# First product of the first FFN: twelve column tiles as six units of seven half-size products, and the last gate's adaLN columns computed in the last FFN

## The chip, the cores and the metric

The kernel runs on one core of a Trainium2 chip, in one launch. The metric is device time in microseconds of that core. The median of three runs of the kernel before is 1328.9 us (1328.61 to 1329.11).

## The reference, cut to what matters

A sequence of 512 tokens with 1024 features passes two layers. Each layer is a token mixer (a short convolution in layer 0, an SSD mixer in layer 1) followed by a SwiGLU FFN. All four sub-layers have RMSNorm before and after, and a shift, a scale and a gate that come from the condition vector `c`:

```python
mod = (jax.nn.silu(c) @ ada_w + ada_b).reshape(bsz, DEPTH, 2, 3, D_MODEL)
...
shift, scale, gate = (mod[:, i, 1, k][:, None, :] for k in range(3))
h = rmsnorm(x, norm_g[i, 2]) * (1.0 + scale) + shift
y = swiglu_ffn(h, f_w_in[i], f_w_out[i])
x = x + gate * rmsnorm(y, norm_g[i, 3])

def swiglu_ffn(h, w_in, w_out):
    gate, up = jnp.split(h @ w_in, 2, axis=-1)
    return (jax.nn.silu(gate) * up) @ w_out
```

`w_in` of an FFN is 1024 x 5632: 22 gate tiles and 22 up tiles of 128 columns. `ada_w` is 1024 x 12288; its last 1024 columns (from `88 * P`) make the gate of the last FFN.

## The kernel before, in words

**Numbers.** Every large product is float32 made of three matmuls. An operand is split into a rounded part ("hi", ScalarE: `act.copy` into float32r) and the rest ("lo", VectorE: a subtraction), and the product is hi*hi + hi*lo + lo*hi. A weight tile of 128 columns (1024 x 128) costs one hi of 128x1024 and one lo of 128x1024, and, as a plain product (`in_chunk`, `mm_chunk`, `mm3`, L279 to L281), 8 k-tiles x 3 = 24 matmuls of 128x512.

**First FFN, first product** (L1152 and on; `up`, `gate`, `load_pair`). Six column tiles are begun while `h` is being formed and ended by `rest(0..5)`. Then a loop over k = 0 to 37 computes one column tile at a time: `load_pair` loads two tiles with one DMA of 1 MB two rounds ahead, `in_chunk(ws[k], h)` is its 24 matmuls, `gate` is a Silu on ScalarE, `up` multiplies on VectorE, `splits[k + 2]` makes hi and lo of the tile after next, and `sums(n)` runs n steps of the adaLN sums. A finished row tile lies in `raw`; `low_parts` forms sums of halves for the second product.

**adaLN columns.** The columns of `ada_w` that are not needed at the start are summed on VectorE beside the products. `ada_begin(n)` takes n sets of 512 columns, each in four loads of 512 KB (`ada_load`, `SP` queue, three buffers). `sums(1)` is one step: `ada_madd` (L125 for the first of a set, L127 for the others), one multiply-add of 128x512; a set has eight, and after them one `ada_fold` (L134). After each pair of sets a small matmul with `four`, four short additions into `mods`, and for gates `put_gates` (a transpose, a copy, a DMA to memory). The first FFN takes 14 sets, so 112 steps; the last two are the gate of the last FFN.

**Last FFN, first product** (L1840 to L2190). It already has the form that the change brings to the first FFN. Tokens are halved into two times 256, the 1024 rows into two times 512, and two neighbouring column tiles form a unit: a 2x2 by 2x2 product of halves, done with seven products in place of eight. A product is 4 k-tiles x 3 = 12 matmuls of 128x256 (L1920). Even units are gate tiles, odd ones up tiles. A unit u has four weights:

- X: the first column tile, 8 k-tiles; used by P1 and P2.
- Y: sums of the column tiles' halves (`sg`, partly added by DMA, partly by `sum_y`); used by P5 and P6.
- Z: the second tile less or plus other halves (its sum by DMA); used by P7 and P4.
- S: a half-size sum (`sum_s`); used by P3.

Each has its hi on ScalarE (L1875) and its lo on VectorE (L1876). `fetch(u)` issues four or five loads on `SP` (L1859 to L1865) and two accumulating DMAs on `POOL` (`add_`, L1852): of `sg`, then of the Z part of the unit before. `tq` holds the token halves' sums, made once from `h` (`value`, `t_hi`, `t_lo`, `t_four`).

The order of one unit on PE, with v = u - 1, is P1(u), P7(v), P5(u), P2(u), P4(v), P6(u), P3(u). Beside it VectorE runs, in this order: `c12(v)` (L1937, and L1939 for odd v), lo of X(u+1), `c22(v)` (L1946), in some units one `s13` (L1827, L1828), `c11(u)` (L1933), lo of Z(u), `sum_y(u+1)` (L1899), `sum_s(u+1)` (L1903), for odd v the product of `c21` (L1954), lo of Y(u+1), lo of S(u+1). ScalarE runs the hi parts, the copies out of PSUM (L1930) and the Silu's (L1942 for even v, between `c12(v)` and hi of X(u+1)). `c22(v)` reads the PSUM bank A of unit v between P7(v), which it follows, and P4(v), which adds to the same bank: P4(v) waits for it.

**The order is written by hand.** Both parts stand under `tc.manual_schedule` for PE, SP, ScalarE, VectorE and GpSimd: each engine issues its instructions in the order of the code, and a waiting instruction holds all that stand behind it on that engine. The buffers: `wst_p` two (staged weights), `whl_p` four (split weights), four PSUM banks `mm_ps` (A and C of the units) and four `aux_ps` (B).

**The end** (L2200 to L2310). The second product of the last FFN runs over `parts`; `behind(n)` (L2230 and on) does what follows product n: at 31 it multiplies two tiles by the gate (`gated`, L2219), at 33 it reads the two A banks (L2246) that the next product overwrites.

Of the kernel before, what the change touches and what calls it, by code (L numbers as in the profile page):

```python
# [16 lines left out]
P = 128  # L17
# [21 lines left out]
def trunk_kernel(  # L39
# [89 lines left out]
    ada_p = []  # L129

# [441 lines left out]

    ada_sets = []
    for q0 in (16, 0 + 24, 8 + 24, 16 + 24, 48, 56, 64, 72, 80, 88):
        ada_sets += [q0 * P, q0 * P + 512]
# [4 lines left out]
    with ExitStack() as ph:  # L580
# [5 lines left out]
        pool.tensor_tensor(four[:, 0:64], ident[:, 0:64], ident[:, 64:128], ADD)  # L586
        pool.tensor_tensor(four[:, 64:96], four[:, 0:32], four[:, 32:64], ADD)
        pool.tensor_copy(four[:, 0:32], four[:, 64:96])
        pool.tensor_copy(four[:, 32:64], four[:, 64:96])
        pool.tensor_copy(four[:, 96:128], four[:, 64:96])  # L590
# [378 lines left out]
        ffp = ph.enter_context(tc.tile_pool(name="ffp", bufs=NF - NS, reuse_waits="tile"))  # L969
        st_p = ExitStack()  # L970
        sa = st_p.enter_context(tc.tile_pool(name="sa", bufs=1, reuse_waits="tile"))
        wx = [sa.tile([P, 2, 2, T], F32, tag=f"wx{u}", name="w2x") for u in range(3)]
        s1t = sa.tile([P, NS // 2, 256], F32, tag="s1t", name="s1t")
        raw = [sa.tile([P, 4, T], F32, tag=f"raw{q}", name=f"raw{q}") for q in (3, 2, 1, 0)][::-1]
        lead_p = []
# [32 lines left out]

        def up(f, pst):
            g = gates[f]  # L1010
            if f < NS:
                dve.tensor_mul(raw[f // 4][:, f % 4, :], pst, g)
                if f % 4 == 3:
                    p = f // 2 - 1
                    lows.append(lambda: dve.tensor_tensor(a_("s1", p, 2), a_("a21", p, 2), a_("a22", p, 2), SUB))
                    lows.append(lambda: dve.tensor_tensor(a_("a21", p, 2), a_("a11", p, 2), a_("a21", p, 2), SUB))
                return
            a = acts[f] = ffp.tile([P, 2, T], F32R, tag="a", name=f"ff{f}")
# [4 lines left out]
        def low_parts():  # L1023
            while lows:
                lows.pop(0)()

# [125 lines left out]
        with tc.manual_schedule(engines={PE_ENGINE, mybir.EngineType.SP, mybir.EngineType.Activation,  # L1152
                                         mybir.EngineType.DVE, mybir.EngineType.Pool}):
            load_pair(0)
            madds = ada_begin(14)
            for i, f in ((0, 0), (2, 0), (1, 1), (3, 1), (4, 2), (5, 3)):
                rest(i)
                if i in (2, 3):
                    up(f, lead_ps[i])
                    sums(1)  # L1160
                    low_parts()
                else:
                    gate(f, lead_ps[i])
                sums(1)
# [3 lines left out]
            tiles = []  # L1168
            last = 2 * NF - 7
            for k in range(last + 1):  # L1170
                if k % 2 == 0 and k < 2 * NF - 10:
                    load_pair(k // 2 + 1)
                if k in (16, 20, 24):
                    x_load((k - 16) // 4)
                if k in (last - 2, last - 1):
                    xy_load(n_s - 2 + k - last + 2)
                tiles.append(in_chunk(ws[k], h))
# [3 lines left out]
                if j < 2 and k > 2:  # L1181
                    gate(4 + 2 * q + j, tiles[k - 1])
                elif k:
                    up(2 + 2 * q + j, tiles[k - 1])
                if k + 2 < len(splits):
                    for op in splits[k + 2]:
                        op()
                low_parts()
                sums(4 if j < 2 else 3)
                if k == 2 * NF - 12:  # L1190
                    ggs.append(make_gg(1, gg_tile))
                if k == last - 1:
                    assert next(madds, None) is None and not ada_sets and not quarters
# [12 lines left out]
            up(NF - 1, tiles[-1])  # L1206
            for step in todo:
                list(step)
            rows_g = [put_gates(q, mm_ps) for q in (2, 3)]
            for step in rows_g:  # L1210
                next(step)
# [15 lines left out]
            for q, item in enumerate(seq):  # L1227
# [6 lines left out]
                if q in (0, 5):  # L1234
                    list(rows_g[q // 5])
# [532 lines left out]
    with ExitStack() as ph:  # L1768
# [66 lines left out]
        def up(f, pst):  # L1835
# [5 lines left out]
        LO, HI = HALVES  # L1841
        FACTORS = {"P1": ("X", 0, "A"), "P2": ("X", 4, "B"), "P3": ("S", 0, "C"), "P4": ("Z", 4, "A"),
                   "P5": ("Y", 0, "C"), "P6": ("Y", 4, "A"), "P7": ("Z", 0, "A")}
        staged, wts, banks, outs = {}, {}, {}, {}

        def w1_cols(u, f, kh=None):
            c0 = u % 2 * DFF + (4 + u // 2 * 2 + f) * P
            rows = slice(0, D) if kh is None else slice(kh * T, (kh + 1) * T)
            return w1[rows, c0:c0 + P].rearrange("(k p) f -> p k f", p=P)

        def add_(dst, src):
            pool.dma_start(dst, src, accum_op=ADD)  # L1852

        def fetch(u):

            st, sg = wst_p.tile([P, 16, P], F32, tag="wst", name="wsu"), sums_w[:, u % 2]
            staged[u] = st, sg
            if u < UN:
                dma(sg[:, 0], w1_cols(u, 1, 0))  # L1859
                dma(sg[:, 1], w1_cols(u, 1, 1))  # L1860
            if u:
                dma(st[:, 8:12, :], w1_cols(u - 1, 1, 0))
            dma(st[:, 0:8, :], w1_cols(u, 0))
            if u:
                dma(st[:, 12:16, :], w1_cols(u - 1, 1, 1))  # L1865
            if u < UN:
                add_(flat2(sg[:, 0]), flat2(sg[:, 1]))
            if u:
# [462 lines left out]
```

## Time and profile before

| what | value |
|---|---|
| median of three runs | 1328.9 us |
| the profiled execution, its own time | 1328.93 us |
| its span, first to last instruction | 1327.1 us, clock 0.999 |
| PE busy | 1313.8 us, 99% of the span |
| VectorE busy | 1028.0 us, 77% |
| ScalarE busy | 641.5 us, 48% |
| first FFN, six begun tiles and loop | from about 229 to about 451 us |
| last FFN, its units | from 1029.88 us |

The profile is one execution recorded on the chip. PE is TensorE's matmuls, PEld its weight loads, DVE VectorE, ACT ScalarE, POOL GpSimd, SP the engine that issues most DMAs. Matmuls overlap each other, so the distance between two starts, not a matmul's own length, is what one costs; for the other engines too, the next start can lie a little ahead of an end. An entry in brackets tells how long the engine stood idle before the instruction and what ended the wait.

### The profile page before, as it was taken

Reading aid. Unit: us, or ns where it says so; the run is one execution under the profiler, and the core shown is the slowest. Engines: PE = TensorE matmul, PEld = TensorE weight load, DVE = VectorE, ACT = ScalarE, POOL = GpSimd, SP = SyncE. Lnnn points to the kernel's source line nnn. Section 1 sums busy time; section 2 is a strip of 40 time slices with the busy share of each in tenths; the row PEclk is TensorE's granted clock in tenths of the full one; section 3 lists DMA queues with packets and bytes.
Section 4 is the critical chain, followed back from the end, with each engine's and each line's share of the span. In section 5 each row is a group of like instructions: output and inputs, shape, how many; then the busy total and the mean of one; then the engine's idle time right before and its main releaser. Section 6 shows DMA issues by size and latency. Waiting matters only on the chain.

```text
span 1327.1 us, 19226 instructions
## 1 busy us (share of the span) xinstructions
PE 1313.8 (99%) x7437; PEld 1134.4 (85%) x7437; DVE 1028.0 (77%) x1654; ACT 641.5 (48%) x1042; POOL 85.9 (6%) x106
## 2 busy tenths in 40 slices
PE   8999999999999999999999999999999999999997
PEld 7788889888888888898888888888789999998886
DVE  5588866788776686769998989888678777766897
ACT  5322357222222465665554555554574555544665
POOL 0000000000000140000000000000000111101320
PEclk9999999999999999999999999999999999999999
DMA  9757760688885692414534243413252788878961
GB/s 312 230 191 226 247 228 1 214 267 259 286 292 195 178 180 65 130 34 147 159 111 134 74 143 112 143 64 127 85 154 53 190 216 209 200 194 287 177 119 64
DMA packets 203456, 222.21 MB, mean 167 GB/s; under 512 B 8788, under 2 KB 148964, under 8 KB 202340
## 3 DMA queue, kind: packets, MB, share of 16 engines
q1 hardware_dynamic: 186496, 184.74, 44.7%
q0 software_dynamic: 12720, 23.34, 10.2%
q10 hardware_dynamic: 4148, 12.90, 3.0%
q8 instruction: 58, 0.95, 0.3%
q14 instruction: 34, 0.28, 0.1%
HBM read 195.37 MB, written 2.24 MB: 149 GB/s over the span
## 4 chain that ended last, share of the span: by engine, by line
PE 93%; DMA 2%; SPq 2%; DVE 1%; ACT 1%; issue 1%; DVEq 0%; ACTq 0%
PE ip L279 15%; PE ip L281 14%; PE ip L280 14%; PE y L381 8%; PE sA L1920 7%; PE cA L2015 4%; PE cA L1127 3%; PE sC L1920 3%; PE li L279 3%; PE li L281 3%; PE li L280 3%; PE sB L1920 2%; PE li L767 1%; PE yd L1512 1%; PE cC L2015 1%; PE cD L2015 1%
## 5 line engine op out<-in xcount | busy, mean ns | idle before, releaser
L279 PE MATMUL ip<-h,whl 128*128 128x512 f32 x840 | 331.6, 395 | 0.2 <-DVE cv L874 0.2
L281 PE MATMUL ip<-h,whl 128*128 128x512 f32 x840 | 327.6, 390 | 0.0
L280 PE MATMUL ip<-h,whl 128*128 128x512 f32 x840 | 327.4, 390 | 0.0
L279 PEld LDWEIGHTS ip<-h,whl 128*128 128x128 f32 x840 | 157.8, 188 | 33.7 <-issue 1.8
L281 PEld LDWEIGHTS ip<-h,whl 128*128 128x128 f32 x840 | 157.7, 188 | 33.2
L280 PEld LDWEIGHTS ip<-h,whl 128*128 128x128 f32 x840 | 157.9, 188 | 31.7
L225 DVE TENSOR_TENSOR whl<-wst,whl 128x1024 fp32r<-128x1024 f32 x99 | 120.4, 1221 | 41.6 <-ACT whl L224 41.5
L224 ACT CAST whl<-wst 128x1024 fp32r<-128x1024 f32 x99 | 102.3, 1042 | 61.2 <-DMA wst<-in_f_w_in_dram 49.9
L127 DVE SCALAR_TENSOR_TENSOR ada_acc<-ada_st,csil,ada_acc 128x512 f32<-128x512 f32 x140 | 105.0, 750 | 21.5 <-DMA ada_st<-in_ada_w_dram 18.1
L381 PE MATMUL y<-whlo,ys 128*128 128x512 f32 x384 | 89.4, 392 | 0.0
L381 PEld LDWEIGHTS y<-whlo,ys 128*128 128x128 f32 x384 | 71.8, 188 | 15.8 <-issue 0.7
L279 PE MATMUL li<-h,whl 128*128 128x256 f32 x288 | 83.4, 290 | 0.0
L281 PE MATMUL li<-h,whl 128*128 128x256 f32 x288 | 81.7, 284 | 0.0
L280 PE MATMUL li<-h,whl 128*128 128x256 f32 x288 | 81.6, 283 | 0.0
L1920 PE MATMUL sA<-tq,whl 128*128 128x256 f32 x576 | 74.6, 284 | 0.3 <-DVE g L1946 0.3
L1920 PEld LDWEIGHTS sA<-tq,whl 128*128 128x128 f32 x576 | 71.6, 192 | 0.6 <-DVE g L1946 0.5
L1366 DVE SCALAR_TENSOR_TENSOR cu<-ip,cols,cu 128x511 f32<-128x511 f32 (+2 forms) x84 | 62.8, 747 | 4.0 <-ACT cu L1363 1.4
L2015 PE MATMUL cA<-whlo,ao 128*128 128x512 f32 x264 | 61.0, 391 | 1.2 <-ACT whlo L1980 1.0
L2015 PEld LDWEIGHTS cA<-whlo,ao 128*128 128x128 f32 x264 | 49.3, 188 | 12.3 <-ACT whlo L1980 2.0
L1876 DVE TENSOR_TENSOR whl<-wsu,whl 128x1024 fp32r<-128x1024 f32 x33 | 40.4, 1223 | 23.4 <-ACT whl L1875 23.4
L279 PEld LDWEIGHTS li<-h,whl 128*128 128x128 f32 x288 | 55.3, 192 | 0.0
L280 PEld LDWEIGHTS li<-h,whl 128*128 128x128 f32 x288 | 55.3, 192 | 0.0
(371 smaller groups left out, 2319.5 us busy)
## 6 DMA issues: line engine op xcount, KB each, us to landing
ada_st<-in_ada_w_dram SPq DMA_DIRECT2D x96, 512.0 KB, 5.9
wst<-in_f_w_in_dram SPq DMA_DIRECT2D x26, 1024.0 KB, 7.2
wst<-in_m_w_in_dram SPq DMA_DIRECT2D x14, 1024.0 KB, 5.4
wst<-in_m_w_in_dram SPq DMA_DIRECT2D x20, 512.0 KB, 6.0
wst<-in_a_w_in_dram SPq DMA_DIRECT2D x9, 1024.0 KB, 6.8
wsu<-in_f_w_in_dram SPq DMA_DIRECT2D x17, 512.0 KB, 5.5
csb<-cs_d ACTq DMA_DIRECT2D x8, 1024.0 KB, 6.5
sg<-in_f_w_in_dram SPq DMA_DIRECT2D x32, 256.0 KB, 3.4
```

Of the source, the lines that this page charges most:

```text
L127: dve.scalar_tensor_tensor(acc, w, csil[:, k:k + 1], acc, MUL, ADD)
L224: later.append((lambda sw=sw, w=w: act.copy(w[:, 0, :nk, :], sw), lambda sw=sw, w=w: dve.tensor_tensor(w[:, 1, :nk, :], sw, w[:, 0, :nk, : ...
L225: lambda sw=sw, w=w: dve.tensor_tensor(w[:, 1, :nk, :], sw, w[:, 0, :nk, :].bitcast(F32), SUB)))
L279: pe.matmul(dst, w_at(w, 0, kk), a[:, 0, sl], start=start, stop=False)
L280: pe.matmul(dst, w_at(w, 0, kk), a[:, 1, sl], start=False, stop=False)
L281: pe.matmul(dst, w_at(w, 1, kk), a[:, 0, sl], start=False, stop=stop)
L381: pe.matmul(pst, a[:, al, tk], wt[:, wl, kk, :], start=k == 0 and i == 0, stop=k == K - 1 and i == 2, skip_group_check=bool(held))
L1127: pe.matmul(bank[r, sub], a[:, al, q, tk], w[:, wl, q, :], start=first and k == 0, stop=False, skip_group_check=True)
L1366: dve.scalar_tensor_tensor(u[:, sft:], pst[:, :T - sft], w[3 - sft], u[:, sft:], MUL, ADD)
L1876: dve.tensor_tensor(dst[:, 1], src, dst[:, 0].bitcast(F32), SUB)
L1920: pe.matmul(dst, w[:, wl, k0 + k, :], moving(q, k, al), skip_group_check=True, start=q in ("P1", "P5", "P2") and k == 0 and i == 0, stop=k ...
L2015: pe.matmul(bank[r][sub], a[:, al, q, tk], w[:, hl, q, :], start=first and k == 0, stop=last and k == 2, skip_group_check=True)
```

## The change

It makes the functions of the last FFN's units into two classes, `Units` and `Values`, and uses them in the first FFN for the column tiles 4 to 9 of gate and up (12 tiles, 6 units, `UN1 = 6`); tiles 10 to 21 stay plain. In the first FFN each unit also holds two adaLN steps (`sums(1)` after `c11` and after the last split) and `low_parts(1)`; the six begun tiles hold three steps. `ada_begin` takes 12 sets instead of 14 there, and the plain loop runs 4, 4, 4 and 3 steps a tile in place of 4, 4, 3 and 3. The two sets of the last gate move to the units of the last FFN (`gate_late`), in units 2 to 9 two multiply-adds each, between `c11(u)` and the split of Z(u), with their loads on `SP` into a part of `raw`, `make_four` on GpSimd, and in units 10 to 13 the fold's matmul, the additions and `put_gates(3)`. In the end part `gated` moves from 31 to 30. The memory of `ffp` and `sa` is cut anew.

```diff
+    class Units:
+        FACTORS = {"P1": ("X", 0, "A"), "P2": ("X", 4, "B"), "P3": ("S", 0, "C"), "P4": ("Z", 4, "A"),
+                   "P5": ("Y", 0, "C"), "P6": ("Y", 4, "A"), "P7": ("Z", 0, "A")}
...
+        def fetch(self, u):
+            st, sg = wst_p.tile([P, 16, P], F32, tag="wst", name="wsu"), self.sums_w[:, u % 2]
...
-    for q0 in (16, 0 + 24, 8 + 24, 16 + 24, 48, 56, 64, 72, 80, 88):
+    for q0 in (16, 0 + 24, 8 + 24, 16 + 24, 48, 56, 64, 72, 80):
...
+        UN1 = 6
+        ffp = ph.enter_context(tc.tile_pool(name="ffp", bufs=1, reuse_waits="tile"))
...
-            load_pair(0)
-            madds = ada_begin(14)
-            for i, f in ((0, 0), (2, 0), (1, 1), (3, 1), (4, 2), (5, 3)):
-                rest(i)
...
+            madds = ada_begin(12)
+            part_of.fetch(0)
+            rest(0)
+            gate(0, lead_ps[0])
+            for j in range(4):
+                vs.value(j)
...
+            part_of.split_y(0)
+            up(1, lead_ps[3])
+            sums(1)
+            acc.append(in_chunk(more[1], h))
+            part_of.sum_s(0)
+            part_of.split_s(0)
+            up(2, acc[0])
+            vs.four(0)
+            sums(2)
...
+            for u in range(UN1):
+                v = u - 1
+                end = u == UN1 - 1
+                if not end:
+                    un.fetch(u + 2)
...
+                un.product(u, "P1")
+                if u:
+                    un.c12(v)
+                else:
+                    vs.four(1)
+                    up(3, acc[1])
+                un.split_x(u + 1)
+                if u:
+                    un.product(v, "P7")
+                un.keep(u, "A", 0, lo_)
+                un.product(u, "P5")
+                if u:
+                    un.c22(v)
+                low_parts(1)
+                un.product(u, "P2")
+                un.keep(u, "C", 1, hi_)
+                if u:
+                    un.product(v, "P4")
+                un.c11(u)
+                sums(1)
+                un.split_z(u)
+                if not end:
+                    un.sum_y(u + 1)
+                    un.sum_s(u + 1)
+                un.product(u, "P6")
...
+                un.product(u, "P3")
+                un.keep(u, "A", 0, hi_)
+                if not end:
+                    un.split_s(u + 1)
+                sums(1)
...
-                sums(4 if j < 2 else 3)
+                sums(3 if j == 3 else 4)
...
+            def gate_late():
+                st = [raw[:, 18 + 2 * b:20 + 2 * b, :] for b in range(2)]
...
+                load(0)
+                yield
+                load(1)
+                for i, (n, kh) in enumerate(quarter):
+                    yield
+                    for k in range(2):
+                        ada_madd(acc, st[i % 2][:, k, :], kh * 2 + k)
+                    load(i + 2)
+                    if kh == 3:
+                        ada_fold(acc, part[:, n * 16:n * 16 + 16])
+                yield
+                yield from ada_fin(88 * P, part)
+                yield from put_gates(3)
...
                 c11(u)
+                next(late, None)
                 split_z(u)
...
-                    elif n == 31:
-                        gated(got["11", t], 0, got["11", t])
+                        if n == 30:
+                            gated(got["11", t], 0, got["11", t])
```

More of the change, by code (lines that the diff above doesn't have):

```diff
@@ new lines, in trunk_kernel @@
+            u = UN1 - 1
+            load_pair(pp)
+            tiles = [in_chunk(un.wts["X", UN1], h)]
+            un.c12(u)
+            for op in splits[3]:
+                op()
+            un.product(u, "P7")
+            gate(fu, tiles[0])
+            sums(2)
+            tiles.append(in_chunk(more_n[0], h))
+            un.c22(u)
+            for op in splits[4]:
+                op()
+            un.product(u, "P4")
+            gate(fu + 1, tiles[1])
+            sums(3)
+            load_pair(pp + 1)
@@ L1851, in add_ @@
[L1851 to L1868, printed above, removed]
-                add_(flat2(st[:, 8:12, :]), flat2(staged[u - 1][0][:, 0:4, :]))
@@ L1960, in trunk_kernel @@
+        fetch, product, keep = part_of.fetch, part_of.product, part_of.keep
+        split_x, split_y, split_z, split_s = part_of.split_x, part_of.split_y, part_of.split_z, part_of.split_s
+        sum_y, sum_s, wts = part_of.sum_y, part_of.sum_s, part_of.wts
+        c11, c12, c21, c22 = part_of.c11, part_of.c12, part_of.c21, part_of.c22
         even = list(range(NP))
```

409 lines of the change are left out of this document (261 added, 148 removed).

## The prediction

> **What bounds the kernel now.** I read the page's busy shares first (the table above), then the chain that ended last, then the table by stage, then the order of time in the stages that the change touches.
>
> ```profile
> PE 93%; DMA 2%; SPq 2%; DVE 1%; ACT 1%; issue 1%; DVEq 0%; ACTq 0%
> ```
>
> PE is busy for 99% of the span and carries 93% of the chain, so time is won only by fewer or faster matmuls, and lost only where PE is made to wait. The plain loop of the first FFN and the units of the last, in the table by stage (columns: PE, PEld, DVE, ACT, POOL busy, clock, DMA share, GB/s):
>
> ```profile
> 300.00:320.00 20.00, 20.00 (x90) 16.59 (x90) 15.86 (x23) 5.07 (x6) 0.00 (x0) 1.00 0.87 270
> 1080.00:1100.00 20.00, 20.00 (x169) 20.00 (x168) 15.35 (x22) 10.56 (x18) 3.46 (x4) 1.00 0.85 211
> ```
>
> PE stops in neither; VectorE has 4 to 5 us of 20 free. One plain column tile is read from two Silu's on ScalarE, each of which waited for the end of its tile:
>
> ```profile
> 258.80 0.60 ACT L1000 ACTIVATE g<-ip 128x512 f32<-128x512 f32 x1 [6.35 <-PE ip L281]
> ...
> 264.24 0.60 ACT L1000 ACTIVATE g<-ip 128x512 f32<-128x512 f32 x1 [3.91 <-PE ip L281]
> ```
>
> A tile costs 264.24 - 258.80 = 5.44 us, or 226.7 ns for each of its 24 matmuls. The unit that the change copies into this stage is seen in the last FFN, unit 6 on PE:
>
> ```profile
> 1088.02 1.60 PE L1920 MATMUL sA<-h,whl 128*128 128x256 f32 x12
> ...
> 1098.10 1.60 PE L1920 MATMUL sA<-h,whl 128*128 128x256 f32 x12
> ```
>
> From P1 of unit 6 to P1 of unit 7 there are 10.08 us for 84 matmuls, 120 ns each and 1.44 us a product.
>
> **The gain on PE.** Two plain tiles are 2 x 5.44 = 10.88 us, a unit is 10.08 us: 0.80 us won. Six units: **-4.8 us**. This is all that the change can win in the first FFN; the 26 other column tiles stay as they are (the loop's steps go from 14 to 15 in four tiles, which VectorE's free 4 us of 20 hide).
>
> Seven products for eight should win 12.5%, and win 7%, because a 128x256 matmul takes more than half of a 128x512 one. The Trainium skill, "TensorE: Matmul & The Clock Gate", section "Back-to-back issue gap", gives N/2.4 + 2.5 ns, so 109 and 216 ns; an estimate by that page would be 48 x 216 - 84 x 109 = 1.2 us a unit and -7.3 us in all. The trace has 120 and 226.7 ns for these matmuls, and the rows decide.
>
> **The price: VectorE's chain in a unit.** The units of the last FFN run with PE full, but just so. Here is VectorE from `c11` of unit 6 on (1094.05) to `c22` of unit 6 (1103.33), which runs in unit 7, then ScalarE in the gap before 1102.19, then P4(6) on PE:
>
> ```profile
> 1094.05 0.42 DVE L1933 TENSOR_TENSOR g<-sB,g 128x256 f32<-128x256 f32 x1 [1.04 <-PE sB L1920]
> 1095.11 1.22 DVE L1876 TENSOR_TENSOR whl<-wsu,whl 128x1024 fp32r<-128x1024 f32 x1 [0.64 <-ACT whl L1875]
> 1096.25 0.69 DVE L1899 TENSOR_TENSOR sg<-sg,wsu 128x512 f32<-128x512 f32 x1
> ...
> 1099.53 0.68 DVE L1876 TENSOR_TENSOR wss<-wsu,wss 128x512 fp32r<-128x512 f32 x1
> 1100.13 0.42 DVE L1937 TENSOR_TENSOR g<-sC,g 128x256 f32<-128x256 f32 x1
> 1102.19 1.23 DVE L1876 TENSOR_TENSOR whl<-wsu,whl 128x1024 fp32r<-128x1024 f32 x1 [1.63 <-ACT whl L1875]
> 1103.33 0.42 DVE L1946 SCALAR_TENSOR_TENSOR g<-sA,g 128x256 f32<-128x256 f32 x1
> ```
>
> ```profile
> 1100.59 0.63 ACT L1942 ACTIVATE g<-g 128x512 f32<-128x512 f32 x1 [1.44 <-DVE g L1937]
> ```
>
> ```profile
> 1103.85 1.41 PE L1920 MATMUL sA<-tq,whl 128*128 128x256 f32 x10
> ```
>
> The chain begins where P2(6) ends on PE (`c11` and hi of Z wait for it), and from 1095.11 it has no free time (the three rows left out, `sum_s`, `c21` and lo of Y, have no idle entry): each step follows the one before, through Silu and hi of X on ScalarE, to `c22`, which ends at 1103.75; P4(6), which waits for it, starts at 1103.85. **The slack is 0.1 us in a pair of units.** In the first such pair it was below zero; the trace shows PE's one stall of this stage, by `c22` (L1946):
>
> ```profile
> 1043.28 2.90 PE L1920 MATMUL sA<-tq,whl 128*128 128x256 f32 x22 [0.28 <-DVE g L1946]
> ```
>
> The two gaps that the chain does have are the 0.64 us before lo of Z, and, where v is even, the 1.63 us in which VectorE waits for ScalarE; nothing added is placed in the second. From `c22` of an odd unit the way is free: it ends 1.4 us ahead of P4(5) at 1093.78 in this row.
>
> ```profile
> 1034.47 0.42 DVE L1933 TENSOR_TENSOR g<-sB,g 128x256 f32<-128x256 f32 x1 [1.15 <-PE sB L1920]
> ...
> 1091.99 0.42 DVE L1946 SCALAR_TENSOR_TENSOR raw<-sA,raw 128x256 f32<-128x256 f32 x1
> ```
>
> What the change puts into this chain are adaLN steps. Their prices:
>
> ```profile
> 252.75 0.75 DVE L127 SCALAR_TENSOR_TENSOR ada_acc<-ada_st,csil,ada_acc 128x512 f32<-128x512 f32 x1 [1.55 <-DMA ada_st<-in_ada_w_dram]
> 253.42 0.68 DVE L1012 TENSOR_TENSOR raw<-ip,g 128x512 f32<-128x512 f32 x1
> ...
> 257.26 0.71 DVE L134 TRANSPOSE_TENSOR_REDUCE fold<-ada_acc 128x16 f32<-128x512 f32 x1
> 257.90 0.45 DVE L125 TENSOR_SCALAR ada_acc<-ada_st,csil 128x512 f32<-128x512 f32 x1
> ```
>
> From start to start a step takes 253.42 - 252.75 = 0.67 us, a fold 0.64, the first step of a set about 0.45.
>
> **First FFN.** Unit by unit, with steps counted from 1:
>
> - *Units 0 and 1.* The six begun tiles hold steps 1 to 3: 0.45 + 0.67 + 0.67 = 1.8 us. Unit 0 has one `low_parts` more than its pattern (0.6 us, as the 128x512 subtractions in the rows). In the pattern VectorE had 1.15 us free before `c11(0)` (1034.47, the first row of that fence). So `c11(0)` is 1.8 + 0.6 - 1.15 = 1.25 us late. Lo of Z(0) followed `c11(0)` without a gap, so step 4 adds 0.67, and step 5, before `c12(0)`, 0.67: `c22(0)` comes 2.6 us later than in the pattern. There P4(0) waited already, so PE pays **2.5 us** (part of it earlier, at P5(1), which needs Y(1) from the same queue).
> - *Units 2 and 3.* Step 8 and its fold stand in the 0.64 us gap: 1.31 - 0.64 = 0.67. Step 9, a first one, before `c12(2)`: 0.45. Less 0.1 of slack: **1.0 us** at P4(2).
> - *Units 4 and 5.* Step 12 in the gap: nothing or 0.03. Step 13 before `c12(4)`: 0.67. Less the slack: **0.6 us** at P4(4).
>
> Together **+4.1 us**. What stands behind a delayed `c22` on VectorE is `c11`, lo of Z and so on, all for PE; the chain begins anew at the next even unit's P2, so delays don't add up beyond the sum. On ScalarE the same Silu and copies shift with it. On SP a load of a set follows every second step; the fetch of the next unit stands behind it, but is not due before that step has run.
>
> **Last FFN.** Units 2 to 9 get two steps each between `c11(u)` and lo of Z(u), 1.34 us (1.12 where a set begins, units 2 and 6), against the gap of 0.64. In the even units this lands in the tight chain: 4 x 0.7 less 2 x 0.22 less 4 x 0.1 = 2.0 us. Odd units have the 1.4 us of lead that `c22` of an odd unit has before its P4, and bear two steps; in units 5 and 9 a fold comes on top (0.7 + 0.64 = 1.34 of 1.4), and the `s13` behind makes the next `c11` late by what I put at 0.15 each. **+2.3 us.** The small matmul, the transpose and the copies for the gate only change places. `make_four` on POOL stands behind the first accumulating DMA and ahead of the second fetch's; the sum of `sg` that it can delay is read by `sum_y(1)` behind `c11(0)` at 1034.47, over 10 us after the units' weights are begun, so I cost it at nothing.
>
> **End part.** `gated` moves ahead by one product. Around it:
>
> ```profile
> 1299.70 1.23 DVE L1981 TENSOR_TENSOR whlo<-w2t,whlo 128x1024 fp32r<-128x1024 f32 x1 [1.49 <-ACT whlo L1980]
> ...
> 1301.17 1.29 DVE L2219 TENSOR_TENSOR c<-c,w2h 128x512 f32<-128x512 f32 x2
> ...
> 1304.11 1.28 DVE L2246 TENSOR_TENSOR w2h<-w2h,cA 128x512 f32<-128x512 f32 x2
> ```
>
> ```profile
> 1304.94 1.40 PE L2015 MATMUL cA<-whlo,ao 128*128 128x512 f32 x5 [0.99 <-ACT whlo L1980]
> ```
>
> PE's largest stall in the stage is the 0.99 us before 1304.94. The bracket names a ScalarE split, but the next product overwrites the A banks that L2246 reads, and the first L2246 ends about 0.15 us before PE starts: that is the wait, I think. The two L2219 cost VectorE 1.2 us in front of it. Before 1299.70 VectorE is idle for 1.49 us, and there the change puts them. **-0.9 us** (bounds: 0, if ScalarE is the true releaser, and -1.0).
>
> **DMA.** Each unit that holds steps moves 512 KB more. In the units the DMA share is 0.85 (the row of 1080 to 1100). Landing times in three places (kind, count, size, us): in the units, alone before them, and in the first FFN's second product beside 512 KB loads:
>
> ```profile
> wsu<-wsu POOLq DMA_DIRECT2D x13, 256.0 KB, 4.2
> ```
>
> ```profile
> sg<-sg POOLq DMA_DIRECT2D x2, 256.0 KB, 3.6
> ```
>
> ```profile
> w2y<-w2x POOLq DMA_DIRECT2D x6, 256.0 KB, 5.8
> ```
>
> So an accumulation can land 1.6 us later than now (5.8 - 4.2), or not at all later. One that is issued in unit 6 is read by hi of Z in unit 7:
>
> ```profile
> 1095.04 0.86 POOL L1852 DMA_DIRECT2D wsu<-wsu  x1 [0.19 <-issue]
> ```
>
> ```profile
> 1104.36 1.05 ACT L1875 CAST whl<-wsu 128x1024 fp32r<-128x1024 f32 x1
> ```
>
> 1104.36 - 1095.04 - 0.86 - 4.2 = 4.3 us lie between its landing and its reader. That holds one such delay and more, so I take **0** and keep +1.0 us for each loaded unit as the other end.
>
> **Sum.** -4.8 + 4.1 + 2.3 - 0.9 = +0.7 us. The profiled execution took 1328.93 us in all, 1.8 us more than its span; it stands on the median (1328.9). Forecast: **1329.6 us**.
>
> **The rivals.**
>
> 1. *Slower: the loop of fetches becomes the bound.* A fetch waits for the accumulation into Z of the unit before, since that reads the staging buffer that it reuses; load, accumulate and load again go round once in a unit; I take the round, as the worst case, to be as long as PE's unit already, 10.08 us. If each loaded unit adds 1.0 us to the round, the eight loaded units of the last FFN need 8.0 us more, of which PE's own delay (2.3) and the 4.3 us before hi of Z take 6.6 and leave 1.4; in the first FFN six loaded units need 6.0 against 4.1 + 1 (it starts with less lead): 0.9. Together +2.3: 1331.9 us. At the whole 1.6 us it is 8 x 0.6 + 6 x 0.6 = 8.4 more. It decides from the point where an accumulation lands over 0.8 us later in each loaded unit (6.6 / 8). For it: the share of 0.85 and the row of 5.8. Against it: while a fetch waits, the loads of `sg` ahead of it go on, so the round shortens. The Trainium skill, "DMA: Bandwidth & Descriptors", section "SWDGE vs HWDGE vs iDMA", says that each DMA engine takes turns between its queues; by that rule a load on SP's queue beside an accumulation on POOL's would slow it, as this rival has it. The rows of 3.6, 4.2 and 5.8 us agree in direction. Chance 0.30.
> 2. *Faster: VectorE finds more room than I give it.* If the backlog of units 0 and 1 costs 1.0 rather than 2.5, because short waits for ScalarE in the begun tiles take up the steps, and the other pairs half: 1.0 + 0.8 + 1.1 = 2.9 instead of 6.4, so 1326.1 us. For it: VectorE waited for ScalarE in several places before unit 0; against it: the steps are not placed in those waits. Chance 0.22.
> 3. *The products are not cheaper.* Weight loads already fill PEld in the units; were a 128x256 matmul beside this stage's traffic 130 ns in place of 120, a unit would cost 10.92 us and win nothing: 1334.4 us. Nothing in the trace shows such a change. Chance 0.03.
>
> The forecast itself has 0.45 and its own range, 1328.0 to 1331.3.
>
> **How the numbers follow.** A difference under 0.2%, 2.7 us, can hardly be told from none here. The range reaches to 1325.8 (most of rival 2) and 1334.0 (rival 1 with some of its upper bound, since a quarter of it lies above). Faster by over 0.2% (below 1326.2): about half of rival 2 and some of a larger gain in the end part, 0.20. Slower (above 1331.6): most of rival 1, rival 3 and the upper edge of the forecast, 0.33. Same: 0.47.
>
> **What would show it.** In the changed profile: six units of 84 matmuls with 10.08 us between P1's where nothing waits; PE stalls by `c22` in units 1, 3 and 5 of the first FFN, of some 2.5, 1.0 and 0.6 us, and four to six of 0.3 to 0.7 us between units 3 and 10 of the last; no stall before the product in which L2246 stood. If the stalls are put down to DMA or to splits whose staging was late, rival 1 is at work. If units 1, 3 and 5 show hardly any stall, rival 2. If the stall before 1304.94 stays, the end part was misread.

## The result and the profile after

The changed kernel takes 1345.5 us in the median of four runs (1345.21 to 1347.06), the kernel before 1329.0 beside it: ratio 1.0127, 95% interval 1.011 to 1.0145. It is **16.5 us slower**, far above the predicted 1329.6 and outside the range (1325.8 to 1334.0). The profiled execution took 1345.36 us with a span of 1343.5. Line numbers have moved: a unit's product is L654 (was L1920), its copy out of a bank L664, `c22` L681, the split's lower part L617 (units) and L231 (plain tiles), the fold L140, and in the first FFN's second product `a_prep` is L1290 and L1291, `w_prep` L1281 and L1282, the product L1310.

The chain that ended last, on the page of the kernel after:

```profile
PE 76%; DVE 11%; DMA 7%; ACT 3%; issue 2%; SPq 2%; DVEq 0%; ACTq 0%; POOLq 0%
```

It was 93% PE; VectorE has 11% of it now and DMA 7%. The table of what PE waited for (us in all, times, longest) says where:

```profile
PE sA L654 <- DVE g L681: 4.0, 6, 1.3
...
PE sA L654 <- ACT g L664: 2.5, 2, 2.2
PE ada_ps L147 <- DVE fold L140: 2.2, 1, 2.2
PE cA L1310 <- ACT ao L1290: 1.7, 1, 1.7
...
PE cA L1310 <- DVE ao L1291: 1.3, 1, 1.3
...
PE cA L1310 <- DVE whlo L1282: 0.4, 1, 0.4
```

The first row is what the prediction spoke of. The other five are new. In order of time the two traces give this account (starts of the same instructions; the second stretch ends one matmul, 0.23 us, after the start of the last plain one):

| stretch | before, us | after, us | difference |
|---|---|---|---|
| to the ninth column tile of the first FFN | 253.2 | 253.5 | +0.3 |
| the 36 column tiles from there | 197.8 | 201.5 | +3.8 |
| the second product's first bank, `cA` | 11.1 | 21.9 | **+10.8** |
| to unit 0 of the last FFN | 567.8 | 567.7 | -0.1 |
| the 16 units there and the tiles with their last product | 171.3 | 174.2 | +2.9 |
| to the end of the span | 125.9 | 124.7 | -1.2 |

The sum is 16.5 (span 16.4). Two thirds of it stand at a place that the prediction did not look at, the seam between the first FFN's first and second product.

**The seam.** PE of the kernel after, from the last plain tile on:

```profile
454.79 0.39 PE L287 MATMUL ip<-h,whl 128*128 128x512 f32 x1
457.36 0.41 PE L147 MATMUL ada_ps<-fold,four 128*128 128x32 f32 x2 [2.18 <-DVE fold L140]
...
458.46 10.79 PE L1310 MATMUL cA<-whlo,ao 128*128 128x512 f32 x35 [0.35 <-DVE whlo L1282]
470.93 0.73 PE L1310 MATMUL cA<-whlo,ao 128*128 128x512 f32 x2 [1.67 <-ACT ao L1290]
472.92 4.14 PE L1310 MATMUL cA<-whlo,ao 128*128 128x512 f32 x10 [1.26 <-DVE ao L1291]
476.89 11.07 PE L1310 MATMUL cB<-whlo,ao 128*128 128x512 f32 x48
```

And VectorE there (the first line is the last take-up of a tile before the seam; `g<-ip,g` at 459.77 takes up the tile that PE ended at 449.57):

```profile
440.85 0.68 DVE L1201 TENSOR_TENSOR g<-ip,g 128x512 f32<-128x512 f32 x1
...
449.34 3.90 DVE L127 SCALAR_TENSOR_TENSOR ada_acc<-ada_st,csil,ada_acc 128x512 f32<-128x512 f32 x5
455.02 1.54 DVE L127 SCALAR_TENSOR_TENSOR ada_acc<-ada_st,csil,ada_acc 128x512 f32<-128x512 f32 x2 [1.78 <-DMA ada_st<-in_ada_w_dram]
456.59 0.71 DVE L140 TRANSPOSE_TENSOR_REDUCE fold<-ada_acc 128x16 f32<-128x512 f32 x1
457.23 1.18 DVE L1282 TENSOR_TENSOR whlo<-w2x,whlo 128x1024 fp32r<-128x1024 f32 x1
...
459.77 0.69 DVE L1201 TENSOR_TENSOR g<-ip,g 128x512 f32<-128x512 f32 x1
```

In the kernel before, the same split of `w2x` ran at 441.82, 9.2 us ahead of the product, and the last fold at 413.21:

```profile
413.21 0.71 DVE L134 TRANSPOSE_TENSOR_REDUCE fold<-ada_acc 128x16 f32<-128x512 f32 x1
...
441.82 1.23 DVE L1099 TENSOR_TENSOR whlo<-w2x,whlo 128x1024 fp32r<-128x1024 f32 x1 [4.22 <-ACT whlo L1098]
```

Now the last adaLN sums stand in VectorE's queue ahead of the second product's first weights. VectorE reaches the seam 10.2 us late, and PE starves until it has caught up. The waits (2.18, 0.35, 1.67, 1.26) are 5.5 us. Most of the other half of the 10.8 is in the table by stage (PE, PEld, DVE, ACT, POOL, granted clock, DMA share, GB/s):

```profile
340.00:440.00 100.00, 100.00 (x448) 82.76 (x447) 82.65 (x126) 21.45 (x27) 0.00 (x0) 1.00 0.86 282
...
459.00:461.00 2.00, 1.93 (x5) 1.59 (x6) 1.40 (x3) 0.51 (x1) 0.90 (x2) 0.60 1.05 386
461.00:463.00 2.00, 2.00 (x6) 1.52 (x5) 1.60 (x2) 2.00 (x4) 1.05 (x2) 0.54 1.05 387
...
473.00:475.00 2.00, 2.00 (x5) 1.62 (x6) 2.00 (x3) 0.89 (x3) 0.70 (x1) 0.52 0.96 159
475.00:477.00 2.00, 2.00 (x7) 1.52 (x7) 1.97 (x3) 0.50 (x1) 0.00 (x0) 0.63 0.67 116
```

After each of the two gaps the granted clock is near one half for almost 4 us. PE counts as busy there (at most 11 matmuls in 459 to 463, where 17 would fit).

**The units.** From P1(0) at 253.48 to the first plain tile at 319.79 PE ran 40 products, 57.6 us at 1.44; it took 66.3, so 8.7 were lost:

```profile
260.17 1.93 PE L654 MATMUL sA<-tq,whl 128*128 128x256 f32 x12 [2.22 <-ACT g L664]
261.90 2.76 PE L654 MATMUL sC<-h,wss 128*128 128x256 f32 x12
...
272.01 3.14 PE L654 MATMUL sA<-tq,whl 128*128 128x256 f32 x24 [1.20 <-DVE g L681]
...
293.06 3.14 PE L654 MATMUL sA<-tq,whl 128*128 128x256 f32 x24 [0.63 <-DVE g L681]
...
309.50 1.70 PE L654 MATMUL sA<-tq,whl 128*128 128x256 f32 x12 [0.33 <-ACT g L664]
...
315.37 3.14 PE L654 MATMUL sA<-tq,whl 128*128 128x256 f32 x24 [1.29 <-DVE g L681]
```

The stalls by `c22` are in units 1, 3 and 5 as predicted (1.20, 0.63, 1.29: 3.1 us). The last of them is not the steps alone. The split of Z(4), ahead of it in the chain, waited on ScalarE for one of the accumulating DMAs:

```profile
305.14 1.05 ACT L616 CAST whl<-wsu 128x1024 fp32r<-128x1024 f32 x1 [2.78 <-DMA wsu<-wsu]
```

In the traces of ten_sets, pace54 and pace4 below, whose units are the same, this wait is missing, the stall in unit 5 is 0.22 or 0.23, the 0.33 us before 309.50 is missing too, and the stretch takes 64.6 us in place of 66.3. By this comparison about 1.7 us of this execution's 8.7 belong to that one transfer. The largest stall, in unit 0, wasn't foreseen; the row after it shows the half clock again (2.76 us for a product of 1.60; the four products from 260.17 to 267.77 take 7.6 us in place of 5.8). ScalarE shows why P6(0) waited: it needs bank A copied out, and that copy stands behind the second part of the fourth sum and the split of X(1):

```profile
258.28 0.63 ACT L709 ACTIVATE tq<-raw 128x512 fp32r<-128x512 f32 x1 [2.81 <-DVE raw L729]
258.82 1.03 ACT L616 CAST whl<-wsu 128x1024 fp32r<-128x1024 f32 x1
259.75 0.36 ACT L664 COPY g<-sA 128x256 f32<-128x256 f32 x1
```

VectorE wrote that `raw` late, since two adaLN steps (256.11 to 257.56) stood in front.

**Theory:** the units are cheaper on PE as computed, but the adaLN sums no longer have room. Fewer of them run in the units' 66 us, the plain loop is asked for one more in four tiles, VectorE falls behind in it, and the sums reach the seam. **Rivals:** the seam is late because of the units' memory, which holds back the loads of the second product's weights; or the adaLN loads are late, not VectorE; or the moved gate is what costs.

### The profile page after: what moved, and what is told of

It is laid out like the page before. It is cut to its first block, busy times and chain, and to the rows that moved or that the text cites. A ratio compares the mean times of both kernels' runs of the same rounds, so it can differ in the third digit from the quotient of the medians.

```text
span 1343.5 us, 19889 instructions
## 1 busy us (share of the span) xinstructions
PE 1319.2 (98%) x7653; PEld 1145.6 (85%) x7653; DVE 1065.7 (79%) x1717; ACT 662.6 (49%) x1084; POOL 99.7 (7%) x123
## 4 chain that ended last, share of the span: by engine, by line
PE 76%; DVE 11%; DMA 7%; ACT 3%; issue 2%; SPq 2%; DVEq 0%; ACTq 0%; POOLq 0%
PE y L387 10%; PE ip L285 9%; PE ip L287 9%; PE ip L286 9%; PE sA L654 6%; PE cA L2210 4%; DMA ada_st<-in_ada_w_dram 3%; PE sC L654 3%; PE cA L1310 3%; DVE ada_acc L127 2%; DMA wsu<-wsu 2%; PE li L285 2%; PE li L287 2%; PE li L286 2%; PE li L929 1%
## 5 line engine op out<-in xcount | busy, mean ns | idle before, releaser
L285 PE MATMUL ip<-h,whl 128*128 128x512 f32 x744 | 293.7, 395 | 0.2 <-DVE cv L1036 0.2
L287 PE MATMUL ip<-h,whl 128*128 128x512 f32 x744 | 289.9, 390 | 0.0
L286 PE MATMUL ip<-h,whl 128*128 128x512 f32 x744 | 289.6, 389 | 0.0
L285 PEld LDWEIGHTS ip<-h,whl 128*128 128x128 f32 x744 | 139.7, 188 | 29.9 <-issue 1.8
L287 PEld LDWEIGHTS ip<-h,whl 128*128 128x128 f32 x744 | 139.6, 188 | 29.9 <-DVE whl L231 0.4
L286 PEld LDWEIGHTS ip<-h,whl 128*128 128x128 f32 x744 | 139.8, 188 | 28.0
L231 DVE TENSOR_TENSOR whl<-wst,whl 128x1024 fp32r<-128x1024 f32 x86 | 104.3, 1219 | 29.2 <-ACT whl L230 29.2
L654 PE MATMUL sA<-tq,whl 128*128 128x256 f32 x792 | 104.3, 285 | 7.0 <-DVE g L681 4.0
L654 PEld LDWEIGHTS sA<-tq,whl 128*128 128x128 f32 x792 | 98.6, 192 | 10.0 <-DVE g L681 5.7
L230 ACT CAST whl<-wst 128x1024 fp32r<-128x1024 f32 x86 | 89.2, 1042 | 31.0 <-DMA wst<-in_f_w_in_dram 14.7
L127 DVE SCALAR_TENSOR_TENSOR ada_acc<-ada_st,csil,ada_acc 128x512 f32<-128x512 f32 x126 | 94.4, 749 | 11.8 <-DMA ada_st<-in_ada_w_dram 9.2
L617 DVE TENSOR_TENSOR whl<-wsu,whl 128x1024 fp32r<-128x1024 f32 x46 | 56.1, 1220 | 24.9 <-ACT whl L616 24.7
```

What stands on the lines that cost most here:

```text
L127: dve.scalar_tensor_tensor(acc, w, csil[:, k:k + 1], acc, MUL, ADD)
L230: later.append((lambda sw=sw, w=w: act.copy(w[:, 0, :nk, :], sw), lambda sw=sw, w=w: dve.tensor_tensor(w[:, 1, :nk, :], sw, w[:, 0, :nk, : ...
L231: lambda sw=sw, w=w: dve.tensor_tensor(w[:, 1, :nk, :], sw, w[:, 0, :nk, :].bitcast(F32), SUB)))
L285: pe.matmul(dst, w_at(w, 0, kk), a[:, 0, sl], start=start, stop=False)
L286: pe.matmul(dst, w_at(w, 0, kk), a[:, 1, sl], start=False, stop=False)
L287: pe.matmul(dst, w_at(w, 1, kk), a[:, 0, sl], start=False, stop=stop)
```

## The experiments

Ratios are to the kernel before, run on the same chip.

**One half alone.** The first FFN of the kernel before, with the gate's columns in the last FFN and `gated` at 30:

```diff
-for q0 in (16, 0 + 24, 8 + 24, 16 + 24, 48, 56, 64, 72, 80, 88):
+for q0 in (16, 0 + 24, 8 + 24, 16 + 24, 48, 56, 64, 72, 80):
...
+                next(late, None)
```

> The kernel before with one half of the change: the adaLN columns of the last gate computed in the last FFN (twelve sets in the first FFN instead of fourteen) and the gating one product earlier; the first FFN stays plain. Theory (the first FFN lost the time): in the trace of the changed kernel the last FFN's units stretched by 3.0 us and the end part shrank by 1.3, so 1329.0 + 3.0 - 1.3 = 1330.7 us, with short stalls of PE by the second difference (c22) in the last FFN and none at the first FFN's second product. Rival (the moved columns are the larger cost, through the fetches of the last FFN): 1334 us or more.

1330.76 us, ratio 1.002 (1.0011 to 1.0029): as expected. The half that was moved costs 2.1 us, so 14.5 of the 16.5 belong to the units in the first FFN and to what they do to its sums. The third rival falls.

**The gating alone:**

```diff
-                    elif n == 31:
-                        gated(got["11", t], 0, got["11", t])
+                        if n == 30:
+                            gated(got["11", t], 0, got["11", t])
```

> The kernel before with only the gating of the first two row tiles moved ahead by one product in the last FFN. If the stall of 0.99 us in the end part is the wait for the A banks, as predicted: 1329.0 - 0.9 = 1328.1 us, at most -1.3. If ScalarE is the true releaser: 1329.0 us.

1327.76 us, ratio 0.9994 (0.9985 to 1.0003): 0.95 us less in the medians, about the size computed, though the interval includes no change. In the trace the stall is gone; what PE still waited for in the end part is this:

```profile
PE cA L2015 <- DVE c L2244: 0.2, 1, 0.2
PE cA L2015 <- DVE w2h L2246: 0.2, 1, 0.2
```

So the releaser was VectorE, as argued, and not ScalarE, whose name stood in the bracket.

**Two sets fewer:**

```diff
-            madds = ada_begin(12)
+            madds = ada_begin(10)
```

> The changed kernel without the last two of the twelve sets of adaLN columns in the first FFN (the scale of the last FFN is left at a constant), so that the sums end some 16 steps, over 20 us, before the plain loop does. Theory (the sums reach the loop's end, hold the space and the engines that the second product needs, and the waits of 5.5 us there bring a half clock of another 5 us): 1345.5 - 10.5 = 1335 us, no stall of PE between the loop and the second product, clock 1.00 there. Rival (the units' memory makes the second product's weights late): still above 1342 us, with stalls at the same place.

1332.63 us, ratio 1.0028 (1.0016 to 1.004), 12.9 us less than the changed kernel. The seam is whole, at clock 1.00:

```profile
453.16 11.17 PE L1311 MATMUL cA<-whlo,ao 128*128 128x512 f32 x48
464.16 11.04 PE L1311 MATMUL cB<-whlo,ao 128*128 128x512 f32 x48
```

The units and all their memory are as in the changed kernel, so the first rival falls: the seam is the sums' doing.

**No step in the units:**

```diff
-            madds = ada_begin(12)
+            madds = ada_begin(8)
...
-            sums(1)
...
-            sums(2)
...
-                sums(1)
```

> The changed kernel with no adaLN step ahead of and in the six units of the first FFN, and eight sets in place of twelve (shift and scale of the last FFN are left at constants); its sums too end well before the loop. Theory (besides the loop's end, the steps in the units' chain on VectorE cost the 4.0 us of stalls by c22, and the two steps ahead of unit 0 most of the 2.2 us stall in unit 0 with its half clock): 1345.5 - 10.5 - 3.5 - 3.0 = 1328.5 us. Rival (the units of this stage stall for their weights or by their own order, whatever the adaLN steps do): about 1335 us, the time of the kernel with ten sets.

1329.5 us, ratio 1.0011 (1.0001 to 1.0021), with four sets fewer. From unit 2 on every unit takes 10.08 us. So the stalls by `c22` in units 3 and 5 go with the adaLN steps and their loads. Units 0 and 1 still lose time without them, by their own order:

```profile
263.12 1.70 PE L656 MATMUL sA<-tq,whl 128*128 128x256 f32 x12 [0.82 <-ACT g L666]
...
268.24 3.14 PE L656 MATMUL sA<-tq,whl 128*128 128x256 f32 x24 [0.55 <-DVE g L683]
```

**ScalarE's order in unit 0:**

```diff
                 else:
+                    un.keep(u, "A", 0, lo_)
                     vs.four(1)
```

> The changed kernel with one instruction moved on ScalarE: in unit 0 the copy out of bank A comes before the parts of the fourth sum and the split of X(1), so P6(0) needs not wait for them. Theory (the 2.2 us stall in unit 0 is ScalarE's order behind VectorE's late sums, and its half clock costs 1.5 more): the stall goes and part of it comes back where P1(1) waits for X(1), so 1345.5 - 3 = 1342.5 us. Rival (the fetch of unit 1 is what is late, so the stall moves on to P1(1) whole): 1345 us.

1343.62 us, ratio 1.0114 (1.0097 to 1.0131): 1.9 us less than the changed kernel, not 3, and the two intervals overlap. The stall moved on to P3(0) (0.8 us) and P7(0), which waits for the second copy out of bank A, and that copy stood behind a split too:

```profile
PE sA L654 <- ACT g L664: 2.9, 1, 2.9
```

The stretch from P1(0) to the first plain tile takes 64.6 us here, and as long in ten_sets and pace54, which don't have this edit. So it is not shown that this order wins anything by itself.

**A faster loop.** The steps that the loop takes in four tiles, first 5, 5, 4, 4, then 4, 4, 4, 4:

```diff
-                sums(3 if j == 3 else 4)
+                sums(5 if j < 2 else 4)
```

> The changed kernel with all twelve sets, but the loop of plain tiles takes 5, 5, 4, 4 adaLN steps in four tiles instead of 4, 4, 4, 3, so that the sums end some 14 steps earlier in the program, about 3 tiles before the loop does. Theory (it is the sums that reach the loop's end, not the work itself, that costs 11.2 us there): 1345.5 - 11.2 = 1334.3 us. Rival (the loop can't take more, because the loads or VectorE are full at 15 steps in four tiles): above 1340 us, with the last sum still at the loop's end or PE waiting inside the loop.

1346.12 us, ratio 1.013 (1.0115 to 1.0145): nothing won; **my expectation failed**. The sums do end before the seam, and PE waits inside the loop instead, for weights whose split stands behind them on VectorE:

```profile
PE ip L287 <- DVE whl L231: 5.4, 6, 2.6
...
PE ip L285 <- ACT whl L230: 2.4, 3, 1.1
```

```diff
-                sums(3 if j == 3 else 4)
+                sums(4)
```

> The changed kernel with 4 steps in every tile of the loop instead of 4, 4, 4, 3: four or five steps earlier, one tile before the loop's end. Theory: VectorE's backlog of about 10 us at the second product shrinks by one tile, 5.4 us, and the waits of PE and their half clock with it, more than in proportion: 1336 to 1340 us. Rival (the place of the last sum doesn't matter, only their number): 1345 us.

1342.28 us, ratio 1.0096 (1.0079 to 1.0114), less than expected too: 2.5 us still in waits for `ao` at the seam, 1.8 us in the loop. The profiled execution was the shortest of the four (1337.93 us; the others 1342.16 to 1343.78), so these waits are the least that this kernel has. So it isn't only where the last sum stands: the loop can't carry them.

**Which half of a sum is too much, its load or its step?**

```diff
-                    dma(st, ada_w[kh * 256:(kh + 1) * 256, c0:c0 + 512].rearrange("(k p) f -> p k f", p=P))
+                    dma(st[:, 0, :], ada_w[kh * 256:kh * 256 + P, c0:c0 + 512])
...
-                        ada_madd(acc, st[:, k, :], kh * 2 + k)
+                        ada_madd(acc, st[:, 0, :], kh * 2 + k)
```

> The changed kernel with every load of adaLN columns cut to its first half, 256 KB, which both of its steps read (the sums are thereby over half of the rows, twice); VectorE's work is unchanged. In the loop of the changed kernel VectorE waited 13.6 us for these loads in five places, and by the loop's end was 10 us late. Theory L (the loads, which arrive 5.4 us after their issue, make VectorE late): the waits go, VectorE is in time at the loop's end, the 11.2 us there go: 1334 us. Theory V (VectorE's own work of some 19 us in four tiles and 3.3 us of waits for ScalarE, against 21.8 us of PE, make it late): most of the lateness stays, 1339 us or more.

1338.13 us, ratio 1.0072 (1.0058 to 1.0085). VectorE's waits for loads between 320 and 460 us fell to 1.3 us (12.1 in the changed kernel by the same view), and it is still late at the seam: the last fold at 448.06 instead of 456.59, PE waiting 2.8 us for `ao`:

```profile
DVE whl L231 <- ACT whl L230: 10.8, 9, 1.6
...
DVE ada_acc L125 <- DMA ada_st<-in_ada_w_dram: 1.3, 1, 1.3
```

```diff
-                        ada_madd(acc, st[:, k, :], kh * 2 + k)
+                        if not k:
+                            ada_madd(acc, st[:, k, :], kh * 2 + k)
```

> The changed kernel with every second adaLN step left out (the sums miss half of the rows); the loads are unchanged. Theory V: VectorE is in time in the loop, the 11.2 us at its end go, and the stalls of the units shrink by about 2: 1332 us. Theory L: the loads come as late as before, and the last sum still ends at the loop's end: 1340 us or more.

1332.35 us, ratio 1.0025 (1.0015 to 1.0036): no loss at the seam, although VectorE waits as long for loads (12.2 us). The time was between the two theories in the first run and at theory V's in the second. The second product's first bank takes 21.9 us in the changed kernel, 16.6 with half the loads and 11.2 with half the steps. So the loads make about half of the lateness. VectorE's own work with its waits for ScalarE is enough for the other half, and with half of that work the late loads do no harm.

**Steps in VectorE's gaps.** All steps of both FFNs where VectorE waits: two behind `c12` in odd units, in the first FFN two more ahead of `c11` in units 2 and 4, none ahead of unit 0, the copies out of bank A early, pace 5, 5, 4, 4:

```diff
                 if u:
                     un.c12(v)
+                    if u % 2:
+                        sums(2)
...
                     un.c22(v)
-                low_parts(1)
+                    low_parts(1)
+                    if u % 2 == 0:
+                        sums(2)
...
                 un.c11(u)
-                sums(1)
```

> The whole change, with its adaLN steps placed in the waits that VectorE has in the trace: in both FFNs' odd units two steps behind c12, where VectorE waits 1.63 us for ScalarE, in the first FFN's units 2 and 4 two more ahead of c11 (idle 1.47 us), none ahead of unit 0, 5, 5, 4, 4 in the loop; the two copies out of bank A in unit 0 as early as they can be. Theory (the stalls come from where the steps stand, and without them the units win their 4.8 us): 1328.7 - 4.8 - 1.0 for the end part + 1 for what is left of the stalls of unit 0 and 1 = 1324 us, faster than both kernels. Rival (the steps cost what they cost wherever they stand, as VectorE and the loads are full): 1330 us or more.

1344.0 us, ratio 1.0112 (1.0097 to 1.0127). My expectation failed on the total and held for the units. Ten steps run inside them, and between 250 and 320 us PE waits once:

```profile
PE sA L654 <- DVE g L681: 1.2, 1, 1.2
```

The 7 us won there are lost again in the loop, which takes 152.5 us for the 24 plain tiles in place of 135.2 (10 us are waits for splits); the seam's first bank takes 12.5. With the loop at the change's pace and two sets fewer:

> The kernel of the run slots with the loop's pace of the change (4, 4, 4, 3) and without the last two sets in the first FFN (the scale of the last FFN is left at a constant). In slots the units took their 10.08 us each with one stall of 1.25 us, and the loop then lost what was won. Theory (with steps in VectorE's waits and with room in the loop the units win what the product count says): 1328.7 - 4.8 - 1.0 for the end part + 1.6 for unit 1 + 0.9 for the last FFN = 1325.4 us. Rival (the gain on PE is lost in the loop whatever room it has): 1329 us or more.

1327.56 us, ratio 0.999 (0.9981 to 0.9999). The whole kernel is 1.3 us below the one before and not 3.3, although it leaves out two sets: the splits in the loop still make PE wait 2.1 us. The run that follows has the same late steps and gating, no units, and leaves nothing out. It is 0.3 below, so about 1.0 us is left for the units, and the two intervals overlap. A gain by the units is not shown.

The late gate in the same way, with the first FFN plain:

```diff
                 if u:
                     c12(v)
+                    if u % 2:
+                        next(late)
...
                 c11(u)
-                next(late, None)
+                if last:
+                    next(late)
```

> The run late_gate (first FFN plain, last gate's columns in the last FFN, gating one product earlier) with the late steps moved from behind c11 in every unit to behind c12 in the odd units, where VectorE waits for ScalarE. Theory (late_gate's 3.0 us in the last FFN are the even units' chain): they shrink to 0.9 or less: 1330.8 - 2.1 = 1328.7 us, at best 1327.8. Rival (the loads beside the fetches are the price): 1330.8 us.

1328.54 us, ratio 0.9998 (0.999 to 1.0007), 2.2 us less than with the steps behind `c11`. The tight chain of the even units was the price, not the loads, which are the same eight here.

**Fewer units, the whole computation:**

```diff
-        UN1 = 6
+        UN1 = 4
```

> The whole computation with four units in place of six (eight column tiles), the adaLN steps in VectorE's waits (none in units 0 and 1), all twelve sets, the loop's pace of the change; the loop then has four plain tiles more, and 22 us more for the sums. Theory (the loss is the adaLN work that six units leave no room for): 1328.8 - 3.2 for four units - 1.0 for the end part + 0.7 for unit 1 + 0.9 for the last FFN = 1326.2 us, and up to 2 us more if VectorE is late at the loop's end. Rival (units in this stage lose at any count): 1330 us or more.

> The same with two units (four column tiles), for which the loop has eight plain tiles more than with six. Theory: 1328.8 - 1.6 - 1.0 + 0.7 + 0.9 = 1327.8 us, no lateness at the loop's end. Rival as before: 1330 us.

Four units: 1333.78 us, ratio 1.0033 (1.0021 to 1.0046); the expectation failed, the seam still makes PE wait 2.5 us for `ao` at a clock of 0.83 (460 to 470). Two units: 1328.64 us, ratio 1.0 (0.9991 to 1.0009). With none (late_slots) it is 1328.54, with six (slots, at a quicker pace of the loop) 1344.0. In these four runs the loss grows with the number of plain tiles that the units take away from the sums. No version with the whole computation is shown to be faster than the kernel before.

## Why the prediction was wrong

- *The gain on PE, -4.8.* Right: undisturbed units take 10.08 us and 1.44 us a product in this stage too. The 36 column tiles took 3.8 us more and not less, because 8.7 were lost in the units: 8.7 - 4.8 = 3.9, to 0.1.
- *Stalls by `c22`, +4.1 (2.5, 1.0, 0.6).* The mechanism was right, in the units named; they measured 1.2, 0.6 and 1.3, and where no transfer was late 1.2, 0.6 and 0.2, half of the forecast. Missed was what the two steps ahead of unit 0 do through ScalarE: P6(0) waits 2.2 us for the copy of bank A, and the half clock after it costs about 1.8. I followed VectorE's queue to `c12` and `c22` and left ScalarE's copies as "shift with it". The copies are released by nothing late themselves; they stand behind a split that is.
- *The loop: "the loop's steps go from 14 to 15 in four tiles, which VectorE's free 4 us of 20 hide".* **This step failed, and with it 10.8 of the 16.5 us**, in two ways. First, I counted steps per tile and not steps in all. By 253 us the program of the kernel before has asked for 15 steps and in the next twelve tiles for 42 (3.5 each); the changed one asks for 3 and for 12. Two sets fewer are 16 steps, so 57 - 15 - 16 = 26 more are left for the 24 plain tiles, at 3.75 a tile 7 tiles or 38 us. That is all the cover that the kernel before had: fold at 413.21, product at 451.07. It was in the trace, and I didn't ask how much of it the change uses up. The 4, 4, 4 and 3 steps hold only from the fifth plain tile on; the first four ask for 2, 3, 2 and 4. In the program the last step so stands in the 23rd of the 24 plain tiles, right ahead of the first split for the second product. Second, the free time in the loop was not free. VectorE of the changed kernel is busy 82.65 us of the 100 from 340 to 440 (the row above; 67.60 in the kernel before), and waits fill most of the rest. From 320 to 460 these are the ones that come with the loop:

```profile
DVE ada_acc L127 <- DMA ada_st<-in_ada_w_dram: 8.9, 4, 4.3
DVE whl L231 <- ACT whl L230: 8.1, 6, 1.6
...
DVE ada_acc L125 <- DMA ada_st<-in_ada_w_dram: 3.2, 1, 3.2
```

  The 1.6 us for ScalarE's half of a split come back with each tile that is taken up into `g`, and no step is placed there. So the loop could not give the time back either, as pace54 shows. Waits for loads alone need not make anything late: the kernel before has 17.2 us of them from 320 to 451, and its sums end 38 us ahead.
- *The seam itself.* What would be late when the sums are late was not named: the first `whlo` and `ao` of the second product, behind them on VectorE. After that a stage follows in which VectorE is busy 9.9 of 10 us (470 to 480), so it can't catch up.
- *Last FFN, +2.3.* Right in the main: +2.9 in the trace, and late_slots shows the chain of the even units as the cause. In units 3 to 10 there are six delays of 0.27 to 0.55 us. Four are at P4 after even units, 1.6 us in all against 2.0 forecast. Two are at P7 after the units with a fold, which wait for a copy on ScalarE, 0.95 us against 0.3.
- *End part, -0.9.* Right: -1.2 in the trace, 0.95 in gated30.
- *DMA, 0.* Nearly right, by a wrong limit. Rival 1 was to decide from the point where an accumulation lands over 0.8 us later. Those into Z in the first FFN's units landed after 7.0 us in the median, against 4.6 in bare_units, whose units hold no steps. In slots it was 6.5 us, and units 2 to 5 took their 10.08 all the same. Only the transfer in unit 4 cost PE anything, about 1.7 us in that execution. So rival 1 is not what made the kernel slow: the slower side came true by another mechanism than the one I priced. Rival 3 falls with the 1.44 us a product.

## What to carry to other kernels

Before counting an engine's idle share as cover, subtract the waits that come back in every round and in which nothing of yours is placed. When a change shortens a stage, list the background work that ran beside it, count it in whole, and see where its last piece will stand; a queue that ends 38 us early has 38 us to give and then none. In an engine that runs in order the place of a step counts: in the last FFN the same sixteen steps cost PE 1.0 us in VectorE's regular waits (late_slots) and 2.9 us behind `c11` (the changed kernel).

## What the runs showed of the hardware

A wait of PE can cost twice. After the 2.22 us gap at 257.95 the granted clock was 0.50 in 262 to 264, and the gaps at the seam (2.2 and 0.35; 1.67 and 1.26) each brought 3.5 to 4 us at 0.52 to 0.63, then 1.00 again. The 1.20 us gap before 272.01 brought none. It isn't regular: in half_loads the same gap before P6(0) was 2.23 us and the clock stayed at 1.00. The Trainium skill, "TensorE: Matmul & The Clock Gate", section "Part 1: The HAM clock gate (the "warmup" mystery)", names half rate as the idle state and a free-running window of about 3.4 us for going idle and for coming back. The half rate and the 3.5 to 4 us until full clock agree with the rows; that a gap of 2.2 us is enough does not agree with a whole idle window, and that one run has the half rate and another, after the same gap, has not would fit a free-running one.
